# Context rows' gates of the even layer: one store of 256 reordered columns in place of three

## The chip, the cores and the metric

One core of a Trainium2 chip. The time is that of one execution of the whole program on the device, in microseconds (us); lower is better. The program is float32 throughout; matrix products are made of three float32r products of high and low parts.

## What is computed

The reference is one inference step of a two-layer backbone over 1024 latent tokens and 256 context tokens of width 1024. Cut to the even layer's gates:

```python
def even_ctx(h, w_in, w_out, gq, gk, sink):
    qa, ka, va, ga, qb, kb, vb, gb = even_projections(h, w_in, gq, gk)
    oa = dense_block_attention(qa, ka, va)
    ob = dense_block_attention(qb, kb, vb, sink)
    y = jnp.concatenate([oa * jax.nn.silu(ga), ob * jax.nn.silu(gb)], axis=-1) @ w_out
```

The same stands for the latent tokens (`even_lat`), with rotary positions, a window in mixer B and the cached context keys. The odd layer is a Fourier mixer, gated in the same way. The kernel computes all of it in one launch.

## The kernel before

The 1280 tokens are ten rows of 128: rows 0 to 7 latent, 8 and 9 context. The even layer's output projection and the odd layer work on the tokens in another order than the attention does, the *stored order*: each half of the sequence is folded so that one position stands first and the rest runs backwards. `PLACE` (L43, cut at the rows into `PIECES`, L47) says, for an attention row, which stored columns its tokens become; for row 9 it is `((1153, 0, 127), (1152, 127, 1))`, counted over all 1280 columns: 127 tokens to columns 1 to 127 of stored row 9 and the last one to column 0, read from a buffer that was written backwards.

The gates are made by `gate0(ct, gi, w)` (L869): `ct` is one of eight blocks of 128 gate channels, `gi` one of three groups of tokens (`GROUPS`, L22): rows 0 to 3, rows 4 to 7, and rows 8 and 9, which is `gi == 2`. So there are eight calls with `gi == 2`, one for each channel block. In each, TensorE (PE) makes 24 matmuls into the one bank of the tag "g" (L872, by the helper at L296), ScalarE (ACT) takes tanh of half of it into a buffer `th` of zone h (L874), VectorE (DVE) multiplies (1 + tanh) with the accumulator, by `silu` (L878), into a second buffer `gs` of zone h, and SyncE (SP) stores `gs` to the DRAM tensor `gd[row, channel, ct, token]`. For `gi == 2` the first 128 columns are written as they are and the next 128 backwards, and three transfers take them to `gd`: row 8 (L894, 64 KB), row 9's columns 1 to 127 (L895, 63.5 KB in pieces of 508 bytes) and row 9's column 0 (L896, 0.5 KB in pieces of 4 bytes). For the latent groups (L880 to L890) VectorE writes the columns in stored order at once, and one transfer takes four rows.

Zone h has nine buffers of 512 columns, taken in turn (`take`, `drop`): the one that was dropped the longest time ago is taken next, and its new user waits until the old one's readers, a store among them, have finished. The raw rows of the weights go through the same zone: `load_w` (L338, from the input projection), `out_weights` (L1170, from the output projection, whose high part ScalarE makes at L316 and whose low part VectorE or GpSimd makes at L322).

The gates are filler work. A `Filler` holds them in a queue with costs, and `attend` (L1144) pumps it while it goes through the attention units: for each unit of one 128-query row and two heads it loads queries (`load_q`, L994, from the DRAM tensor `qd`), makes scores (L989, L1061), maxima and exponentials (`soft`: L1023, L1067 on VectorE, L1030 on ScalarE), and for an earlier unit the transposes (L1108), their high and low parts (L316, L1111) and the product with the values (`weigh`, L1114, L1123, L1125). The attention output is stored at L1131, the reciprocal sums by `totals` (L1077 to L1095). Other filler is the fold of the next layer's weights (L592 to L609). The order of the gate calls:

```python
    for i, nm in enumerate(order[:-1]):
        ...
            work += [gate_work(j, c, gi) for c in range(2) for gi in range(3)]
    ...
    for gi in range(3):
        for n, (jj, c) in enumerate([(int(nm[-1]), c) for nm in order[-2:] for c in range(2)]):
            fl_.add(*gate_work(jj, c, gi))
```

So for the first four channel blocks the groups come one after the other, and for the last four the context group comes last, four calls together, with loads of `w_out` around them.

The stored gates are read once, by `proj_in` (L1273): for each stored row it loads the attention output (L1278), the gates (L1281), the reciprocal sums (L1283) and the residual (L1297), on GpSimd's queue or SyncE's, and multiplies them (L1284, L1285). The pairs of rows come in the order `PAIRS` (L68), with rows 8 and 9 last.

The program is written as a stream of operations, and the framework orders the instructions of each engine at build time, by dependencies and a simulated time line (`schedule_with_timeline_sim=True`, L2053); semaphores and waits follow from it.

Of the kernel before, what the change touches and what calls it, by code (L numbers as in the profile page):

```python
# [17 lines left out]
P = 128  # L18
# [128 lines left out]
def hybrid_step(ctx: ExitStack, tc: tile.TileContext, I, O):  # L147
    nc = tc.nc
    pe, act, dve, pool, sp = nc.tensor, nc.scalar, nc.vector, nc.gpsimd, nc.sync
# [13 lines left out]
    def take(tag, shape, dt=F32):  # L163
        tags = (tag,) if isinstance(tag, str) else tag
        z = min((t for t in tags if spare[t]), key=lambda t: spare[t][0])
        i = spare[z].popleft()[1]
        size = 2 if dt == BF16 else 4
        for s in shape[1:]:
            size *= s
        assert size <= 4 * ZONES[z][1]  # L170
        made[0] += 1
        return Buf(z, i, up.tile(list(shape), dt, tag=f"{z}{i}", name=f"{z}{made[0]}", bufs=1))

    def drop(*bufs):
        for b in bufs:
            stamp[0] += 1
            spare[b.zone].append((stamp[0], b.idx))

    def bank(tag, name, dt=F32):
        tag = ALIAS.get(tag, tag)  # L180
        return pp.tile([P, 512], dt, tag=tag, name=name, bufs=BANKS[tag])
# [6 lines left out]
    def next_bank(name):  # L188
        ring.rotate(-1)
        return bank(ring[-1], name)  # L190
# [5 lines left out]
    gd = dr.tile([NT, P, 8, P], F32, name="gd")  # L196
# [92 lines left out]
    def mm3(out, terms, lo=0, hi=None):  # L289
        n = 3 * len(terms)  # L290
        hi = n if hi is None else hi
        i = 0
        for lh, ll, rh, rl in terms:
            for a, b in ((lh, rh), (lh, rl), (ll, rh)):
                if lo <= i < hi:
                    last = pe.matmul(out, a, b, start=i == 0, stop=i == n - 1)  # L296
                i += 1
        return last
# [64 lines left out]
    def wk(w, k, c0, n):  # L363
        h, l = w[k // 4]
        return h[:, k % 4, c0 : c0 + n], l[:, k % 4, c0 : c0 + n]
# [137 lines left out]
    def hcols(gi, k, c0, n):  # L503
        kper, slots = hT[gi]
        h, l = slots[k // kper]
        return h[:, k % kper, c0 : c0 + n], l[:, k % kper, c0 : c0 + n]
# [362 lines left out]
    def gate0(ct, gi, w):  # L869
        t0, n, v = GROUPS[gi]  # L870
        acc = bank("g", f"ga{ct}{gi}")[:, 0 : n * P]
        mm3(acc, [(*wk(w, k, (ct % 2) * P, P), *hcols(gi, k, 0, n * P)) for k in range(8)])  # L872
        th = take("h", (P, n * P))
        act.activation(th.a, acc, AF.Tanh, scale=0.5)  # L874
        gs = take("h", (P, n * P))

        def silu(out, i, x):
            dve.scalar_tensor_tensor(out=out, in0=i, scalar=1.0, in1=x, op0=ALU.add, op1=ALU.mult)  # L878

        if gi < 2:  # L880
            lo = slice(0, 257) if gi == 0 else slice(256, 512)
            hi = slice(257, 512) if gi == 0 else slice(1, 256)
            if gi == 0:
                silu(gs[:, 0:257], th[:, lo], acc[:, lo])
                silu(gs[:, 257:512][:, ::-1], th[:, hi], acc[:, hi])
            else:
                silu(gs[:, 0:1], th[:, 0:1], acc[:, 0:1])
                silu(gs[:, 1:257][:, ::-1], th[:, lo], acc[:, lo])
                silu(gs[:, 257:512], th[:, hi], acc[:, hi])
            sp.dma_start(gd[t0 : t0 + 4, :, ct, :].rearrange("r p n -> p r n"), gs.a.rearrange("p (r n) -> p r n", r=4))  # L890
        else:
            silu(gs[:, 0:P], th[:, 0:P], acc[:, 0:P])
            silu(gs[:, P : 2 * P][:, ::-1], th[:, P : 2 * P], acc[:, P : 2 * P])
            sp.dma_start(gd[8, :, ct, :], gs[:, 0:128])  # L894
            sp.dma_start(gd[9, :, ct, 1:P], gs[:, 128:255])  # L895
            sp.dma_start(gd[9, :, ct, 0:1], gs[:, 255:256])  # L896
        drop(th, gs)

    HZ[0] = S1_H
# [293 lines left out]
    def gate_work(j, c, gi):  # L1193
        return (5.3 if gi < 2 else 2.7, lambda: gate0(2 * j + c, gi, ws[f"g{j}"]))
# [335 lines left out]
    for c in range(4):  # L1530
        wn = load_w(I["w_g1"][c + 1], tags=BIG) if c in (1, 2) else None
        todo = []
        for c2 in range(2):
            ct = 2 * c + c2
# [387 lines left out]
    for n, (c0, w) in enumerate(pieces):  # L1922
        sl = slice(c0, c0 + w)
        acc = next_bank(f"of7{n}")[:, 0:w]
# [136 lines left out]
```

## Time and profile before

| what | value |
|---|---|
| time, median of 3 runs (lowest to highest) | 1180.46 us (1175.72 to 1181.36) |
| time of the profiled execution | 1181.93 us |
| its span, first to last instruction | 1180.1 us |
| TensorE busy | 1151.1 us, 98% |
| VectorE busy | 829.7 us, 70% |
| ScalarE busy | 570.2 us, 48% |
| GpSimd busy | 329.8 us, 28% |
| DMA packets, of these under 512 bytes | 112592, 25946 |
| mean DMA rate | 143 GB/s |

The profile is of one execution. A row of a timeline or of the chain of waits begins with its start and its length in us; a row of a group of instructions gives the line, the engine, the operation, output and inputs, shapes and the count, then the total time in us and the mean in ns of one, then the idle time of the engine before them and what ended it. "SPq" is SyncE, which only issues transfers and waits. PEclk is the granted clock of TensorE as a share of full speed, DMA share the mean busy share of 16 DMA engines.

### The profile page before, as it was taken

The page shows a single profiled execution, that of the slowest core. Times are in us where ns is not written, and L with a number is a line of the kernel's source. Part 1 is how long each engine was busy: PE and PEld are TensorE (multiplying, and loading weights), DVE is VectorE, ACT ScalarE, POOL GpSimd, SP SyncE. Part 2 cuts the span into 40 slices and gives each one's busy share as a digit, 9 for nine tenths or more (in the row PEclk, how much of TensorE's full clock was granted, in tenths as well). Part 3 has the DMA queues.
Part 4 walks back from the last instruction along what each step waited for, and adds up shares of the span by engine and source line. Part 5 has one row for each costly group of instructions (what it writes and reads, how often), then busy time and mean ns, then how long its engine had stood idle before and what let it go on. Part 6 is the DMA issues. An engine that isn't in the chain of part 4 may idle for free.

```text
span 1180.1 us, 22034 instructions
## 1 busy us (share of the span) xinstructions
PE 1151.1 (98%) x8120; PEld 1035.5 (88%) x8120; DVE 829.7 (70%) x1996; ACT 570.2 (48%) x1149; POOL 329.8 (28%) x293
## 2 busy tenths in 40 slices
PE   9998999999999999999999989999999999999997
PEld 8797999999999998899989878887777889998886
DVE  3589787877777776678888877776765962468543
ACT  4343466565656655556666674432363234342211
POOL 2345733512222230010110035365221226200001
PEclk9999999999999999999999999999999999999999
DMA  9977412323532232344352587784214426364321
GB/s 368 371 275 256 129 62 68 97 83 101 151 90 79 77 97 85 94 127 117 78 154 78 158 227 211 232 238 162 90 46 143 151 98 181 100 213 146 125 107 54
DMA packets 112592, 168.80 MB, mean 143 GB/s; under 512 B 25946, under 2 KB 63574, under 8 KB 112484
## 3 DMA queue, kind: packets, MB, share of 16 engines
q1 hardware_dynamic: 109972, 158.74, 42.6%
q0 software_dynamic: 2368, 8.39, 2.4%
q8 instruction: 64, 1.05, 0.4%
q14 instruction: 44, 0.36, 0.1%
q10 hardware_dynamic: 144, 0.26, 0.1%
HBM read 123.19 MB, written 44.16 MB: 142 GB/s over the span
## 4 chain that ended last, share of the span: by engine, by line
PE 70%; DMA 13%; DVE 8%; issue 3%; POOL 2%; ACT 2%; SPq 1%; POOLq 0%; DVEq 0%; ACTq 0%
PE of L296 9%; PE av L1114 9%; PE pt L1108 8%; PE ga L296 8%; PE q L296 8%; PE sL L989 5%; PE u L296 5%; PE g1O L296 3%; PE kv L296 3%; PE sC L989 2%; PE g1E L296 2%; PE oz L296 2%; DMA u<-i_x 2%; DMA wd<-u 2%; PE g1c L296 1%
## 5 line engine op out<-in xcount | busy, mean ns | idle before, releaser
L1111 DVE TENSOR_TENSOR pt<-pt,pt 128x512 fp32r<-128x512 f32 (+1 forms) x264 | 170.9, 658 | 40.5 <-ACT pt L316 39.5
L316 ACT ACTIVATE pt<-pt 128x512 fp32r<-128x512 f32 (+1 forms) x265 | 147.5, 576 | 101.8 <-PE pt L1108 56.2
L1114 PE MATMUL av<-pt,u 128*128 128x256 f32 x1008 | 167.5, 290 | 1.4 <-DVE e L1125 0.8
L1108 PE MATMUL pt<-identr,p 128*128 128x128 f32 x1008 | 157.2, 273 | 1.5 <-ACT p L1030 0.8
L296 PE MATMUL q<-w,u 128*128 128x256 f32 x960 | 145.1, 287 | 0.5 <-ACT e L559 0.5
L1114 PEld LDWEIGHTS av<-pt,u 128*128 128x128 f32 x1008 | 139.1, 190 | 5.0 <-DVE e L1125 1.0
L296 PEld LDWEIGHTS q<-w,u 128*128 128x128 f32 x960 | 127.2, 189 | 5.5 <-ACT e L559 0.7
L1030 ACT ACTIVATE p<-p,nm 128x1280 f32<-128x1280 f32 (+1 forms) x80 | 95.4, 1193 | 68.2 <-DVE p L1023 68.0
L1108 PEld LDWEIGHTS pt<-identr,p 128*128 128x128 f32 x1008 | 119.7, 141 | 8.1 <-ACT p L1030 1.0
L296 PE MATMUL ga<-u,w 128*128 128x512 f32 (+1 forms) x576 | 124.4, 360 | 0.8 <-DVE byp L1085 0.5
L296 PEld LDWEIGHTS ga<-u,w 128*128 128x128 f32 x576 | 93.8, 188 | 15.4 <-ACT pt L316 1.2
L322 POOL TENSOR_TENSOR w<-h,w 128x512 fp32r<-128x512 f32 x38 | 50.0, 1331 | 134.6 <-DVE w L318 106.6
L989 PE MATMUL sL<-u,q 128*128 128x512 f32 x256 | 82.3, 409 | 0.0
L1030 ACT ACTIVATE p<-p,NM 128x640 f32<-128x640 f32 (+2 forms) x80 | 59.2, 740 | 31.5 <-DVE p L1023 31.2
L989 PE MATMUL sC<-u,q 128*128 128x256 f32 x320 | 62.1, 294 | 2.3 <-DMA q<-qd 2.0
L1023 DVE TENSOR_SCALAR_CACHE_REDUCE p<-sL 128x512 f32<-128x512 f32 x64 | 43.8, 685 | 22.3 <-PE sL L989 14.0
L1023 DVE TENSOR_SCALAR_CACHE_REDUCE p<-sL,nm 128x512 f32<-128x512 f32 x64 | 47.7, 745 | 13.9 <-PE sL L989 12.8
L296 PE MATMUL oz<-u,w 128*128 128x512 f32 x192 | 56.4, 399 | 0.4 <-DVE e L1125 0.4
L759 POOL TENSOR_TENSOR h<-h,rope 128x512 f32<-128x512 f32 (+1 forms) x18 | 21.6, 1199 | 121.4 <-ACT h L842 79.2
L989 PEld LDWEIGHTS sC<-u,q 128*128 128x128 f32 x320 | 48.8, 189 | 5.9 <-issue 2.6
L322 POOL TENSOR_TENSOR u<-h,u 128x512 fp32r<-128x512 f32 x16 | 21.0, 1323 | 109.1 <-ACT u L316 81.2
L296 PE MATMUL of<-u,u 128*128 128x512 f32 x150 | 48.2, 393 | 0.0
(735 smaller groups left out, 2590.7 us busy)
## 6 DMA issues: line engine op xcount, KB each, us to landing
q<-qd SPq DMA_DIRECT2D x80, 256.0 KB
h<-i_w_in SPq DMA_DIRECT2D x40, 256.0 KB
h<-i_w_out SPq DMA_DIRECT2D x32, 256.0 KB
p<-i_ada_s SPq DMA_DIRECT2D x11, 512.0 KB
qd<-pt SPq DMA_DIRECT2D x20, 256.0 KB
qd<-q SPq DMA_DIRECT2D x18, 256.0 KB
w<-i_wuT SPq DMA_DIRECT2D x8, 512.0 KB
u<-i_x SPq DMA_DIRECT2D x8, 512.0 KB
```

Of the source, the lines that this page charges most:

```text
L296: last = pe.matmul(out, a, b, start=i == 0, stop=i == n - 1)
L316: return act.activation(out, in_, AF.Copy)
L322: return pick("lo" + lc, lc).tensor_sub(dst_l, src, dst_h)
L759: pick("rope", XE["rope"]).tensor_mul(t1.rearrange("p t h (b c) -> p t (h b) c", b=2), y.rearrange("p t h (b c) -> p t (h b) c", b=2), cb)
L989: pe.matmul(ps, q_at(q, s, hc), keys, start=s == 0, stop=s == 1)
L1023: dve.tensor_scalar(p[i][:, end[i] : end[i] + n], ps, sign, last[i], op0=ALU.mult, op1=ALU.min, accum_out=c)
L1030: act.activation(p[i][:, 0 : end[i]], p[i][:, 0 : end[i]], AF.Exp, bias=last[i], scale=-1.0, accum_out=SU[:, t, hd + i, 0:1],)
L1108: pe.transpose(tp[:, jj * 256 + i * P : jj * 256 + i * P + P], p[i][:, off : off + P], ident)
L1111: dve.tensor_sub(pt[:, 1, 0:n], tp[:, 0:n], pt[:, 0, 0:n])
L1114: pe.matmul(acc, vv, pt[:, s, jj * 256 : jj * 256 + 256], start=c + jj + s == 0, stop=c + jj == nt - 1 and s == 1,)
```

## The change

For the context group VectorE writes the second 128 columns in stored order: column 128 of the accumulator, which belongs first, by an instruction of one column, and columns 129 to 255 backwards behind it. `gs` then holds rows 8 and 9 as `gd` does, and one transfer of 128 x 2 pieces of 512 bytes (128 KB) stores both. Nothing else is edited.

```diff
         else:
             silu(gs[:, 0:P], th[:, 0:P], acc[:, 0:P])
-            silu(gs[:, P : 2 * P][:, ::-1], th[:, P : 2 * P], acc[:, P : 2 * P])
-            sp.dma_start(gd[8, :, ct, :], gs[:, 0:128])
-            sp.dma_start(gd[9, :, ct, 1:P], gs[:, 128:255])
-            sp.dma_start(gd[9, :, ct, 0:1], gs[:, 255:256])
+            silu(gs[:, P : P + 1], th[:, P : P + 1], acc[:, P : P + 1])
+            silu(gs[:, P + 1 : 2 * P][:, ::-1], th[:, P + 1 : 2 * P], acc[:, P + 1 : 2 * P])
+            sp.dma_start(gd[8:10, :, ct, :].rearrange("r p n -> p r n"), gs[:, 0:256].rearrange("p (r n) -> p r n", r=2))
         drop(th, gs)
```

## The prediction

> **What bounds the kernel now.** I read the page's totals first, then the busy time by stretches, then the waits of TensorE, then the chain of waits where TensorE idles, and last SyncE's issues in that place.
>
> ```profile
> span 1180.1 us, 22034 instructions
> PE 1151.1 (98%) x8120; PEld 1035.5 (88%) x8120; DVE 829.7 (70%) x1996; ACT 570.2 (48%) x1149; POOL 329.8 (28%) x293
> L894 SPq DMA_DIRECT2D gd<-h x4: 326/477/592, 476.1 to 564.1; - x4
> L894 SPq DMA_DIRECT2D gd<-h x4: 319/346/403, 669.5 to 690.0; - x4
> ```
>
> TensorE (PE) is busy for 98% of the span, so a saving elsewhere is worth something only where TensorE idles. The last two rows are the store of L894, asked for in two windows: of the eight blocks that the change touches, four store between 476 and 564 us and four between 669 and 690 us. The next fence gives the busy time of each engine in the first stretch, the second, a part of the second, and the stretch behind it.
>
> ```profile
> core 0: us, PE busy (x) PEld busy (x) DVE busy (x) ACT busy (x) POOL busy (x), PEclk, DMA share, GB/s
> 440.00:660.00 220.00, 218.66 (x1422) 197.18 (x1421) 169.02 (x503) 135.89 (x291) 22.68 (x19) 1.00 0.40 107
> 660.00:710.00 50.00, 45.66 (x337) 42.36 (x336) 39.30 (x126) 34.31 (x86) 13.04 (x15) 1.00 0.71 196
> 692.00:710.00 18.00, 15.98 (x105) 14.54 (x104) 15.27 (x48) 13.96 (x35) 7.86 (x9) 1.00 0.91 244
> 710.00:760.00 50.00, 47.99 (x259) 41.38 (x258) 37.04 (x89) 23.59 (x51) 21.04 (x17) 0.97 0.72 216
> ```
>
> TensorE idles 220.00 − 218.66 = 1.34 us in the first stretch, 50.00 − 45.66 = 4.34 us in the second, and 50.00 − 47.99 = 2.01 us in the fourth. So the first four blocks stand under a full TensorE, the last four beside 4.34 us of idle time. What ends that idle time stands in TensorE's timeline, in brackets:
>
> ```profile
> 663.51 3.02 PE L296 MATMUL ga<-u,w 128*128 128x256 f32 x24 [0.31 <-DVE h L878]
> 680.55 1.64 PE L1114 MATMUL av<-pt,u 128*128 128x256 f32 x9 [0.80 <-DVE e L1125]
> 690.22 1.97 PE L609 MATMUL wa<-h,w 128*128 128x256 f32 x8 [0.39 <-ACT pt L316]
> 702.51 0.47 PE L989 MATMUL sC<-u,q 128*128 128x256 f32 x2 [1.56 <-DMA q<-qd]
> 707.00 0.71 PE L989 MATMUL sC<-u,q 128*128 128x256 f32 x4 [0.46 <-DMA q<-qd]
> ```
>
> The chain of waits shows what stands behind the last four (start, length, what):
>
> ```profile
> 670.35 3.28 DMA gd<-h
> 673.77 5.21 DMA h<-i_w_out
> 679.01 0.03 ACT u L316
> ...
> 684.04 0.47 SPq L896
> 684.56 0.02 SPq L1170
> ...
> 684.61 4.07 DMA h<-i_w_out
> 688.70 0.03 ACT u L316
> ...
> 692.25 9.60 DMA q<-qd
> ```
>
> A buffer of zone h that held gates is used again for raw rows of w_out. The load into it (L1170) waits until the store of the gates has landed, ScalarE stands in its queue at L316 for that load, and the softmax work behind it feeds TensorE late: the 0.80 and the 0.39 us. The 1.56 and 0.46 us belong to query loads (L994). SyncE's issues around it:
>
> ```profile
> 669.50 0.33 SPq L894 DMA_DIRECT2D gd<-h  x1
> 669.92 0.38 SPq L895 DMA_DIRECT2D gd<-h  x1
> 670.35 0.42 SPq L896 DMA_DIRECT2D gd<-h  x1
> ...
> 674.20 0.38 SPq L592 DMA_DIRECT2D w<-i_wuT  x1
> ...
> 680.28 0.32 SPq L896 DMA_DIRECT2D gd<-h  x1
> ...
> 689.95 0.32 SPq L894 DMA_DIRECT2D gd<-h  x1
> 690.36 0.62 SPq L895 DMA_DIRECT2D gd<-h  x1
> 691.04 0.42 SPq L896 DMA_DIRECT2D gd<-h  x1
> 691.55 0.58 SPq L1131 DMA_DIRECT2D od<-e  x1
> 692.25 1.60 SPq L994 DMA_DIRECT2D q<-qd  x2
> ```
>
> **The change part by part.** *VectorE: one instruction more in each of eight blocks.* The second product, 128 columns, becomes one of 1 and one of 127. Rows by shape of L878 between 440 and 710 us (total, mean ns), and the two products of the fifth block in VectorE's timeline:
>
> ```profile
> L878 DVE SCALAR_TENSOR_TENSOR h<-h,ga 128x128 f32<-128x128 f32 x16 | 3.7, 273 | 3.2 <-ACT h L874 3.2
> L878 DVE SCALAR_TENSOR_TENSOR h<-h,ga 128x1 f32<-128x1 f32 x8 | 1.2, 148 | 1.2 <-ACT h L874 1.2
> ...
> 669.19 0.48 DVE L878 SCALAR_TENSOR_TENSOR h<-h,ga 128x128 f32<-128x128 f32 x2
> ```
>
> The 1-column form takes 148 ns by the rows of the latent groups, and 127 columns should cost the 273 ns of 128. That is 8 x 0.148 = 1.18 us of VectorE, which is busy 169.02 of 220 us and 39.30 of 50 us there: it hides beside TensorE's own work. Its cover is gone where the next gate product waits for the single bank that the products read; that happened once, for 0.31 us (at 663.51). Bounds: nothing, and 8 x 0.148 = 1.2 us if it were so in every block. I take 4 x 0.07 = 0.3 us, half of each instruction in the second stretch, since it overlaps the neighbours in part.
>
> *SyncE: two issues fewer in each block.* They last 0.33 to 0.62 us with 0.05 us between them, about 0.43 us each: 16 x 0.43 = 6.9 us of SyncE's time, half of it in the second stretch. In the first stretch this is worth nothing, TensorE having only 1.34 us to give. In the second:
>
> Block at 669.5: the load at 673.77 waited for the third store, issued at 670.35 and 3.28 us under way. The single store can go when the third product is done; the two products end at 669.19 + 0.48 = 669.67, and a third adds about 0.1 us, so its issue falls at about 669.8. Its landing has no row. The nearest are this 0.5 KB store with 3.28 us and the 256 KB loads with 4.07 and 5.21 us. A 128 KB store stands between them in size and is nearest to the store in kind, so I take 3.28: the slot is free at 673.08 and not 673.63, 0.55 us earlier. With 4.07 it is 673.87, a loss of 0.24.
>
> [...]
>
> Block at 677.8: SyncE was held up in it twice, as its own waits between 660 and 712 us show.
>
> ```profile
> SPq L994 <- DMA q<-qd: 2.2, 1, 2.2
> SPq L1170 <- DMA gd<-h: 1.9, 1, 1.9
> SPq L896 <- DMA w<-i_wuT: 0.9, 1, 0.9
> SPq L895 <- DMA h<-i_w_out: 0.8, 1, 0.8
> ```
>
> The stores need nothing of w_uT or w_out. In the issues, the load of w_uT at 674.20 is exactly eight of SyncE's transfers before the store at 680.28: at most eight are under way, and the ninth waits for the first. So each transfer taken out frees a place as well. Nothing on TensorE hung on this block: 0, and not below.
>
> Block at 683.1: the chain goes over the third issue itself (684.04) to the load at 684.61. With one issue instead of three, and a third product ahead of it, the load goes 0.86 − 0.15 = 0.7 us earlier. ScalarE, which waited for it until 688.70, is free that much earlier, and TensorE's 0.39 us at 690.22 goes; the rest of the 0.7 meets no idle time. Gain 0.39, at least 0.
>
> Block at 690: the query loads at 692.25 stand behind three stores and one other. Two issues fewer bring them 0.43 + 0.43 + the odd 0.2 of the long one = about 0.9 us forward, less 0.15 for the product: 0.75. TensorE waited 1.56 us for them; what is late next is the transfer itself, 9.60 us long. In 692 to 710 us the DMA engines are 0.91 busy, so part of an earlier issue is spent in waiting behind GpSimd's row loads, 512 KB each and 9.4 us from issue to landing:
>
> ```profile
> w<-gd POOLq DMA_DIRECT2D x3, 512.0 KB, 9.4
> ```
>
> Bounds 0 and 1.56 + 0.46 = 2.02; I take 0.75.
>
> Sum: −0.55 (of the 0.80) −0.39 −0.75 + 0.3 = −1.39, say −1.4 us. Behind 710 us TensorE is 96% busy again, so what it gains is kept. The profiled execution took 1181.93 us, 1.83 of it outside the span of 1180.1; that gives 1180.5 for it. It lies 1.5 us above the median of the three runs, 1180.46; against the median the forecast is 1179.1.
>
> **The rivals.** *A. As above*: 0.5 to 4 us less, the end at 0.80 + 0.39 + 2.02 + a little more behind it. 1176.5 to 1180.
>
> *B. Hidden altogether.* ScalarE's wait is set by the landing of w_out (5.21 us behind 512 KB of w_uT) and TensorE's by full DMA engines. For it: the 0.91; against it: at 684 the issue itself is the chain. The extra product is left: 1180.46 + 0.3 to + 1.2 = 1180.8 to 1181.7.
>
> *C. All of the idle time comes back.* SyncE waits for the landing of gate stores in other places too, and more places under way ease every transfer in 660 to 760 us; a denser order of work falls out. Then 4.34 + 2.01 = 6.35 us go: 1174.1. Against it: the waits with the large prices (1.56, 0.80) have other transfers behind them. [...]
>
> *D. Slower, by another order of transfers.* The order on each engine is written at build time from simulated readiness, and two transfers fewer and a product more shift it from 476 us on. The price is at 692 to 710 us: the query loads share engines that move 244 GB/s with rows of 512 KB. Each row that gets ahead of them costs 524 KB / 244 GB/s = 2.15 us of TensorE waiting. Three rows ahead cost 6.4 us: 1186.9. From three on it decides; one or two end within 0.5%. For it: nine tenths busy. Against it: GpSimd issues many of these rows on a queue of its own, when buffers come free, not when SyncE does.
>
> **How the numbers follow.** Chances: A 0.55, B 0.18, C 0.15, D 0.12. One measurement of this kernel spreads from 1175.72 to 1181.36, half a per cent, 5.9 us; that is what can be told from no change. C alone reaches past it on the fast side and D alone on the slow side, so faster 0.15, same 0.73, slower 0.12. The likeliest is 1179.1. The range takes in C's 1174.1 and most of D: 1173 to 1185.5; A's own range is 1176.5 to 1180, widened by the spread of the runs.
>
> **What would show it.** L895 and L896 have gone and one store stands in their place, eight times; L878 has eight instructions more, 16 of one column in all; transfers issued by SyncE are 16 fewer. The step at 669.5 is right if the w_out load behind it is issued about 3.4 us after the store's own issue; wrong if the store takes 4 us or more. The step at 690 is right if the query load behind it follows the store at once and TensorE's wait for q falls under 1 us. TensorE's idle time in the 50 us behind the fifth block should be near 3 us. The prediction is wrong if that idle time grows, if a wait of over 2 us for q, scd or od appears on TensorE, or if time is lost where no gate is stored, which would be the order.

## The result: 0.6% slower, and the profile after

The changed kernel takes 1186.36 us, median of 12 runs (1181.34 to 1199.22), beside 1177.89 us for the kernel before in the same session (12 runs, 1175.01 to 1184.29). The ratio is 1.0064, 95% interval [1.0045, 1.0083]; ratios here are of fast runs alone, without the slow one of 1199.22 us, and the two medians as they stand would make 1.0072. Timed once more (run e18 below) the ratio is 1.0069 [1.0043, 1.0095]. The forecast was 1179.1 with a range of 1173 to 1185.5; 1186.36 lies above it, and within 0.6 us of rival D's 1186.9.

The profiled execution took 1193.25 us, 6.9 above the median. First its totals, then its stretches (columns as in the prediction), then the same two late stretches of the kernel before:

```profile
span 1191.3 us, 22014 instructions
PE 1156.4 (97%) x8120; PEld 1041.7 (87%) x8120; DVE 837.2 (70%) x2004; ACT 571.3 (48%) x1149; POOL 328.2 (28%) x293
660.00:710.00 50.00, 42.52 (x305) 39.82 (x304) 37.69 (x122) 31.86 (x77) 10.86 (x12) 0.95 0.66 190
692.00:710.00 18.00, 12.52 (x70) 11.55 (x70) 11.39 (x31) 9.22 (x21) 4.42 (x4) 0.85 0.91 257
710.00:760.00 50.00, 48.25 (x267) 41.52 (x267) 42.72 (x93) 25.79 (x57) 22.58 (x20) 0.99 0.66 195
760.00:810.00 50.00, 50.00 (x269) 42.59 (x268) 42.39 (x73) 18.38 (x48) 29.38 (x16) 1.00 0.73 229
810.00:860.00 50.00, 44.90 (x189) 35.67 (x189) 28.91 (x37) 12.94 (x20) 17.35 (x11) 0.93 0.40 136
```

```profile
760.00:810.00 50.00, 49.62 (x256) 41.37 (x255) 41.22 (x62) 16.12 (x39) 29.83 (x15) 1.00 0.69 206
810.00:860.00 50.00, 49.16 (x228) 39.50 (x226) 32.68 (x50) 18.92 (x36) 22.11 (x16) 1.00 0.39 139
```

TensorE lost time in two places: between 660 and 710 us, where the last four gate blocks lie, and between 810 and 860 us, where no gate is stored. Its waits from 660 to 1000 us, and the timeline rows of the three long ones:

```profile
PE sC L988 <- DMA q<-qd: 6.3, 2, 5.5
PE oz L296 <- DVE w L322: 3.6, 2, 2.1
PE oz L296 <- DVE h L1307: 3.0, 1, 3.0
```

```profile
705.39 0.77 PE L988 MATMUL sC<-u,q 128*128 128x256 f32 x2 [5.48 <-DMA q<-qd]
836.91 0.73 PE L296 MATMUL oz<-u,p 128*128 128x512 f32 x2 [3.01 <-DVE h L1307]
839.74 0.80 PE L296 MATMUL oz<-u,w 128*128 128x512 f32 x1 [2.10 <-DVE w L322]
```

To compare executions I use three marks on TensorE, taken from the records of the trace: the start of its 433rd product for the tile ga (635.6 us before), of its 265th for oz (798.5), and of its 49th for g1E (890.5). The **first place** is the stretch between the first two marks, the **second place** that between the last two. Before they are 162.8 and 92.1 us; in the changed kernel 164.8 and 97.5. That is 2.0 + 5.4 = 7.4 us, near the 7.5 us that 1.0064 makes of 1177.89. (So close an agreement is luck: the first place varies by several us between executions, as the table below shows.) The rest of the profile's surplus, 4.0 us, is there at the first mark already, where the two programs still run the same order: TensorE's granted clock was 0.83 of full speed from 95 to 115 us, against 1.00 (the row of this stretch, before and then after). It is not the change's; in e18, the same program, the first mark stands at 635.2 us.

```profile
95.00:115.00 20.00, 16.84 (x229) 14.78 (x228) 17.49 (x45) 4.94 (x12) 11.15 (x11) 1.00 0.73 245
95.00:115.00 20.00, 16.20 (x202) 14.07 (x202) 14.25 (x41) 5.12 (x12) 7.88 (x8) 0.83 0.62 216
```

The built programs hold the same order on every engine up to about 660 us, and from about 870 us on. Between, 22 places differ on GpSimd, 55 on SyncE, 85 on ScalarE, 161 on VectorE and 603 on TensorE.

### The profile page after: what moved, and what is told of

It is laid out like the page before. It is cut to its first block, busy times and chain, and to the rows that moved or that the text cites. A ratio compares the mean times of both kernels' runs of the same rounds, so it can differ in the third digit from the quotient of the medians.

```text
span 1191.3 us, 22014 instructions
## 1 busy us (share of the span) xinstructions
PE 1156.4 (97%) x8120; PEld 1041.7 (87%) x8120; DVE 837.2 (70%) x2004; ACT 571.3 (48%) x1149; POOL 328.2 (28%) x293
## 3 DMA queue, kind: packets, MB, share of 16 engines
q8 instruction: 64, 1.05, 0.4%
## 4 chain that ended last, share of the span: by engine, by line
PE 80%; DMA 9%; DVE 4%; issue 2%; ACT 2%; POOL 2%; SPq 1%; POOLq 0%; DVEq 0%; ACTq 0%
PE of L296 9%; PE av L1113 9%; PE q L296 9%; PE ga L296 8%; PE pt L1107 8%; PE sL L988 5%; PE oz L296 5%; PE u L296 4%; PE g1E L296 3%; PE g1O L296 3%; PE kv L296 3%; PE sC L988 3%; PE g1c L296 1%; PE sB L1060 1%; DMA q<-qd 1%
## 5 line engine op out<-in xcount | busy, mean ns | idle before, releaser
L296 PE MATMUL q<-w,u 128*128 128x256 f32 x960 | 145.1, 287 | 0.5 <-ACT e L559 0.5
L296 PEld LDWEIGHTS q<-w,u 128*128 128x128 f32 x960 | 127.2, 189 | 5.5 <-ACT e L559 0.7
L296 PE MATMUL ga<-u,w 128*128 128x512 f32 (+1 forms) x576 | 124.2, 360 | 0.3 <-DVE h L878 0.3
L296 PEld LDWEIGHTS ga<-u,w 128*128 128x128 f32 x576 | 93.7, 188 | 14.5 <-ACT pt L316 0.5
L322 POOL TENSOR_TENSOR w<-h,w 128x512 fp32r<-128x512 f32 x38 | 50.1, 1335 | 134.8 <-DVE w L318 105.1
L296 PE MATMUL oz<-u,w 128*128 128x512 f32 x192 | 57.0, 401 | 3.6 <-DVE w L322 3.6
L1022 DVE TENSOR_SCALAR_CACHE_REDUCE p<-sL 128x512 f32<-128x512 f32 x64 | 43.9, 685 | 21.1 <-PE sL L988 12.8
L322 POOL TENSOR_TENSOR u<-h,u 128x512 fp32r<-128x512 f32 x16 | 21.0, 1318 | 108.5 <-ACT u L316 104.2
L296 PE MATMUL of<-u,u 128*128 128x512 f32 x150 | 48.1, 393 | 0.0
```

Source lines behind the costliest of these rows:

```text
L322: return pick("lo" + lc, lc).tensor_sub(dst_l, src, dst_h)
L1022: dve.tensor_scalar(p[i][:, end[i] : end[i] + n], ps, sign, last[i], op0=ALU.mult, op1=ALU.min, accum_out=c)
```

## Experiments

Theory O: the loss is the other build-time order. Theory E: the edit itself costs. To part them, the order of each engine was made a part of the kernel: the instructions of each engine are chained by order-only dependencies in a stored order, that of the kernel before or that of the changed one, whole or in parts. No run times the chaining by itself; e2, chained, loses as much as the changed kernel without it, so the chaining is not what removes the loss.

```diff
+    def keep_order():                       # called at the end of the program
+        ...                                 # chain: one engine's instructions, in the stored order
+            for a, b in zip(chain, chain[1:]):
+                tc.add_manual_dep(
+                    b, a.name, mybir.DependencyInfo(mybir.DependencyClass.NoSync, mybir.DependencyReason.DATA), reason="order"
+                )
```

Line numbers in these kernels are 6 higher for the helpers (L296 is L302, L318 is L324, L322 is L328) and 25 higher in the body (the changed kernel's L1283 is L1308, L1284 is L1309, L1307 is L1332).

| run | edit | order (first part / from about 800 us) | ratio to before, 95% interval | first, second place us | longest wait for q us |
|---|---|---|---|---|---|
| e1 | yes | before / before | 0.9989 [0.9972, 1.0006] | 154.5, 90.2 | 0.4 |
| e2 | no | changed / changed | 1.0077 [1.0052, 1.0103] | 169.7, 98.2 | 6.7 |
| e3 | yes | changed / before | 1.0017 [0.9998, 1.0037] | 158.4, 90.9 | 3.1 |
| e4 | yes | before / changed | 1.0047 [1.0024, 1.0069] | 159.7, 98.1 | 2.9 |
| e5 | yes | before / SyncE changed | 1.0042 [1.0024, 1.0059] | 158.9, 95.4 | 2.5 |
| e6 | yes | before / GpSimd changed | 1.0031 [1.0010, 1.0053] | 159.4, 96.3 | 2.2 |
| e7 | yes | before / VectorE, TensorE, ScalarE changed | 0.9977 [0.9959, 0.9996] | 158.6, 90.3 | 1.9 |
| e8 | yes | SyncE, GpSimd changed / before | 1.0008 [0.9992, 1.0025] | 160.0, 90.8 | 0.5 or less |
| e9 | yes | changed / as e7 | 1.0014 [0.9992, 1.0037] | 160.9, 90.2 | 3.0 |
| e10 | no | as e7 | 0.9986 [0.9964, 1.0007] | 159.2, 89.3 | 1.6 |
| e11 | yes | as e7 | 0.9981 [0.9959, 1.0002] | 155.6, 90.9 | 1.0 |
| e12 | yes | VectorE, TensorE, ScalarE changed / the same | 1.0069 [1.0041, 1.0096] | 166.8, 90.6 | 4.5 |
| e13 | yes | e11 with one move on SyncE | 1.0046 [1.0028, 1.0064] | 157.2, 97.6 | 0.5 or less |
| e14 | yes | e11 with one move on GpSimd | 1.0045 [1.0025, 1.0064] | 162.7, 96.6 | 1.6 |
| e15 | yes | e11 with another move on GpSimd | 0.9985 [0.9968, 1.0002] | 158.1, 91.2 | 1.5 |
| e16 | yes | e9 with one move on GpSimd | 1.0005 [0.9991, 1.0018] | 161.6, 89.8 | 2.6 |
| e17 | yes | changed, but two moves | 1.0005 [0.9985, 1.0026] | 159.0, 91.7 | 3.0 |
| e18 | yes | the changed kernel again | 1.0069 [1.0043, 1.0095] | 161.5, 97.5 | 2.8 |

**The order or the edit: e1 and e2.**

> The edit (one product more, one store for three), with every engine's instructions held in the order that the kernel before has. Theory O (the loss is the other order that the build makes of the program between 660 and 870 us; the edit itself gains what the prediction's steps said): 1 to 2 us less than before, ratio 0.998 to 1.000, and TensorE's wait for the query load near 700 us at 0.5 to 1.5 us. Theory E (the added product or the larger store costs the time in any order): 7 us more than before, ratio about 1.006.

> The kernel before, unedited (two products, three stores), with every engine's instructions held in the order that the changed kernel has. Theory O: 7 to 10 us more than before, ratio 1.006 to 1.009, with a wait of about 5 us on TensorE for the query load near 700 us. Theory E: as before, ratio 0.998 to 1.002.

Medians 1177.6 and 1188.62 us. The edit in before's order loses nothing; the unedited kernel in the changed kernel's order loses all that the changed kernel lost, with its waits (8.8 us for q in all, then 3.1 and 2.1 us at oz) in the same places. Theory E has fallen.

**Which of the two places: e3 and e4.**

> The edit, in the changed kernel's order up to about 800 us and in the order of before from there. By the traces the first part lost 3.9 us in the wait for the query load and 3.4 us in a lower clock behind it, and gave some back later, the second part lost 5 us in waits of the rows 8 and 9 and 3.4 us in the clock. Theory O with the loss in the first part: ratio 1.004 to 1.007; with the loss in the second: 0.998 to 1.001. Theory E: 1.006.

> The edit, in the order of before up to about 800 us and in the changed kernel's order from there. Theory O with the loss in the first part: ratio 0.998 to 1.001; with the loss in the second: 1.004 to 1.007. Theory E: 1.006.

Both count. Against e1, the new order costs 0.28% in the first part alone, little more than the noise of two such timings, and 0.58% in the second alone. The second place is read without doubt, as its stretch scatters little: 98.1 us with the new order there, 90.9 without.

**Which engine in the second place: e5, e6, e7.**

> The edit with the order of before on every engine, except that behind about 800 us SyncE alone issues in the changed kernel's order: there the store of x1d stands ahead of the load of od for row 9. The whole second part in the new order cost 0.58% (1184.1 against 1177.6). Theory S (SyncE's queue makes the loss at 833 us: the load waits in the queue behind a store whose data come late, so row 9's rows land some 6 us later, and everything that uses them follows): 1183 to 1185, ratio to before about 1.0045, and waits of TensorE at oz for VectorE of 3 to 7 us near 833. Theory H (the loss is made where GpSimd, VectorE and TensorE stand in line behind an operation that is not ready): 1177 to 1179, ratio 0.998 to 1.001, no wait of over 1.5 us at oz.

> The edit with the order of before, except that behind about 800 us GpSimd alone works in the changed kernel's order: row 8's product ahead of row 9's, and the small product for the root of rows 4 and 5's squares ahead of the cast that makes row 9's high part. Theory S (SyncE's queue): nothing, 1177 to 1179. Theory H: GpSimd holds row 9's high part back until the small product is ready, VectorE's low part and TensorE's oz for row 9 wait for it: 1180 to 1184, with a wait of 2 to 6 us on TensorE at oz near 833. If only VectorE's and TensorE's order matter, 1177 to 1179 here and the loss in the next run.

> The edit with the order of before, except that behind about 800 us VectorE, TensorE and ScalarE work in the changed kernel's order: VectorE makes row 9's low part (L322) only behind the odd-and-even sums of the pair before and row 8's low part, and TensorE takes the whole product of row 8 ahead of row 9. SyncE and GpSimd as before. Theory S: nothing, 1177 to 1179. Theory H: row 9 was ready first and now waits in VectorE's line for operations that are not ready; TensorE waits at oz for 3 to 8 us near 833: 1181 to 1185.

Against e1's 90.2 us, SyncE's new order alone costs 5.2 us of the stretch, GpSimd's alone 6.1, the three computing engines' nothing. (The stored orders differ there in seven places on SyncE and nine on GpSimd.) Theory S was near for e5, but TensorE's wait was 2.45 us, below its 3 to 7, and the load that it named, row 9's od, is not the one that e13 moves. Theory H was right for GpSimd (e6), but wrong where I held VectorE's order for the cause: e7 in that order is the fastest kernel of all.

**The single moves: e13, e14, e15.** In `proj_in` a row's gates are multiplied with the scaling (scd, the reciprocal sums) and then with the attention output (od); gtd holds the gate rows of the layer's output, x1d the layer's result, and r12y is a reciprocal root made of the squares of an earlier pair of rows. Names with a number are single buffers. On SyncE, the second half of a scaling load (u<-scd, row 9) goes behind three others; on GpSimd, row 8's product goes ahead of row 9's (e14), or the small product r12y ahead of row 9's cast (e15).

```diff
 SyncE (e13)
-u<-scd, second half, row 9
 w<-gtd
 w<-od, row 9
 x1d<-pt
+u<-scd, second half, row 9
```

```diff
 GpSimd (e14)
+w1089: row 8's product
 w1098, p1101, u1116: row 9's product and cast, a low part of w_g
-w1089: row 8's product
 r12y, p1092: the small product, row 8's cast
```

```diff
 GpSimd (e15)
 w1098: row 9's product
+r12y
 p1101, u1116, w1089
-r12y
 p1092
```

> The kernel of e11 with one move on SyncE: the second half of row 9's scaling load (u<-scd) is issued behind the gate-row load, row 9's od load and an x1d store, which stood behind it. In e5 the load went at 803.75 instead of 799.11, and GpSimd's product for row 9 began at 811.86 instead of 803.86. If this move is what e5 showed: TensorE's stretch from oz 265 to g1E 49 is 94 to 96 us (90.3 and 90.9 without it) and the ratio to before about 1.002. If it takes the other moves of e5's order: 90 to 91 us and 0.998.

> The kernel of e11 with one move on GpSimd: row 8's product with od (w1089) stands ahead of row 9's product, cast and the next low part. Row 8's od lands later than row 9's: in e6 GpSimd stood 5.85 us for it. If that is what e6 showed: the stretch from oz 265 to g1E 49 is 93 to 97 us, TensorE waits for row 9's low part or for VectorE at oz for 2 us or more, ratio about 1.002. If the small product for the root (next run) is the cause: 90 to 91 us and 0.998.

> The kernel of e11 with one other move on GpSimd: the small product for the root of a pair's squares (r12y, 0.69 us) stands ahead of the cast that makes row 9's high part. It waits for a sum that follows TensorE's oz of the pair before (r12x, at about 814 us), while row 9 is ready at 810.5. If this is what e6 showed: GpSimd waits 3 to 5 us at r12y, the stretch is 93 to 96 us and the ratio about 1.001. If the swap of the products is the cause: 90 to 91.5 us and 0.998.

One move on SyncE alone costs 97.6 − 90.9 = 6.7 us, one on GpSimd alone 5.7 us; moving r12y costs nothing. The rows show how. GpSimd's timeline in the kernel before (product of row 9 with the scaling, with od, cast), then in the changed kernel:

```profile
810.48 2.41 POOL L1284 TENSOR_TENSOR q<-q,u 128x1024 f32<-128x1024 f32 x1 [7.57 <-DMA u<-scd]
814.54 2.62 POOL L1285 TENSOR_TENSOR w<-w,q 128x1024 f32<-128x1024 f32 x1 [1.65 <-DMA w<-od]
817.22 1.04 POOL L318 CAST p<-w 128x1024 fp32r<-128x1024 f32 x1
```

```profile
823.24 2.39 POOL L1283 TENSOR_TENSOR q<-q,u 128x1024 f32<-128x1024 f32 x1 [13.82 <-DMA u<-scd]
825.59 2.40 POOL L1284 TENSOR_TENSOR w<-w,u 128x1024 f32<-128x1024 f32 x1
827.94 2.40 POOL L1284 TENSOR_TENSOR w<-w,q 128x1024 f32<-128x1024 f32 x1
830.30 0.69 POOL L275 TENSOR_TENSOR r12y<-r12x,mhalf 128x2 f32<-128x2 f32 x1
830.94 2.04 POOL L318 CAST p<-w 128x1024 fp32r<-128x1024 f32 x2
```

And SyncE's issues there, before and then changed:

```profile
802.06 0.49 SPq L1283 DMA_DIRECT2D u<-scd  x1
806.24 1.15 SPq L1283 DMA_DIRECT2D u<-scd  x1
807.49 0.53 SPq L1383 DMA_DIRECT2D w<-gtd  x1
```

```profile
808.03 0.49 SPq L1282 DMA_DIRECT2D u<-scd  x1
812.18 1.21 SPq L1382 DMA_DIRECT2D w<-gtd  x1
813.48 0.38 SPq L1409 DMA_DIRECT2D x1d<-pt  x1
814.22 0.32 SPq L1277 DMA_DIRECT2D w<-od  x1
814.59 0.94 SPq L1282 DMA_DIRECT2D u<-scd  x1
```

The second half goes out 6.6 us behind the first instead of 4.2, and with row 9's od load ahead of it, it is also longer under way: row 9's first product starts 8.65 us after that issue instead of 4.24. So it starts 823.24 − 810.48 = 12.8 us later, 6.8 when the 6.0 us by which everything stood later at the second mark are taken off. In e13 the same move shows alone (issue, then the product that waits for it, 8.45 us later):

```profile
802.19 0.49 SPq L1307 DMA_DIRECT2D u<-scd  x1
810.64 2.40 POOL L1308 TENSOR_TENSOR q<-q,u 128x1024 f32<-128x1024 f32 x1 [14.65 <-DMA u<-scd]
```

Then row 8's product (w<-w,u) stands ahead of row 9's (w<-w,q). Before, row 9's cast ended 817.22 + 1.04 − 810.48 = 7.8 us after the scaling product began; now it is the second of the two casts in the last row and ends 830.94 + 2.04 − 823.24 = 9.7 us after it. That cast is not what TensorE waits for in the end, though. The changed kernel's chain of waits goes from the late products over r12y, which stands behind them on GpSimd:

```profile
830.34 0.66 POOL r12y L275
831.03 1.16 ACT w L1422
832.21 1.85 DVE u L1423
836.17 1.28 DVE h L1307 x2
837.45 2.25 DVE w L322
```

VectorE is idle for 12.28 us before L1423, which needs r12y by way of ScalarE. Behind it in VectorE's order stand L1307, which reads TensorE's accumulator (TensorE's wait of 3.0 us), and row 9's low part, L322 (its wait of 2.1 us), although the cast for that was done at 832.98. The chains of e13 and e14 run the same way. So r12y is a link of the path, and late because of the products ahead of it; e15 says only that its place before the cast does not matter. In e14, where row 9's data are early, GpSimd stands still for row 8's:

```profile
820.18 2.38 POOL L1309 TENSOR_TENSOR w<-w,u 128x1024 f32<-128x1024 f32 x1 [5.61 <-DMA w<-od]
833.44 1.22 PE L302 MATMUL oz<-u,p 128*128 128x512 f32 x2 [3.58 <-DVE h L1332]
```

**The two moves undone in the changed kernel: e9, e17, e18.**

> The changed kernel with its own order on every engine, but for the second part (from about 800 us) on SyncE and GpSimd, where 10 and 8 places are put back as they stood before. Theory Q (the loss at 833 us is made by these two engines alone): TensorE's stretch from oz 265 to g1E 49, 97.5 us in the changed kernel, is 90 to 91 us here, and the time comes back to before's or nearly: ratio 0.998 to 1.002. The rival of it, that the loss needs VectorE's order too, would leave 93 us or more and 1.003 to 1.006. What is left over the repeat of e7 in this call is the price of the first part: 0 if that was chance, 0.2 to 0.3% (2 to 3.5 us) by the runs so far.

> The changed kernel in its own order on every engine, with two moves: on SyncE the second half of row 9's scaling load goes back ahead of the gate-row load, the x1d store and row 9's od load, and on GpSimd row 9's product and cast go back ahead of row 8's product. If these two are the loss near 833 us: TensorE's stretch from oz 265 to g1E 49 is 90 to 91 us instead of 97.5, and the ratio to before 1.000 to 1.002, as e9 had with 18 places put back. If other moves carry a part: 92 us or more, and 1.003 to 1.005.

```diff
 SyncE (e17)
+u<-scd, second half, row 9
 w<-gtd
 x1d<-pt
 w<-od, row 9
-u<-scd, second half, row 9
```

```diff
 GpSimd (e17)
+w1098, p1101: row 9's product and cast
 w1089: row 8's product
-w1098: row 9's product
 r12y, p1092
-p1101: row 9's cast
```

> The changed kernel as it is, once more. By its first timing 1.0045 to 1.0083. Near 700 us, if the new order itself brings TensorE's wait for the query load: 3 to 7 us again; if the 5.5 us were chance: 0.4 to 3 us as in the kernels with before's order there. Near 833 us the stretch from oz 265 to g1E 49 is 97 to 98 us again.

In e9, with both engines' whole second part put back, the second place is 90.2 us and the ratio 1.0014. With these two moves alone put back, the changed kernel's ratio falls from 1.0069 to 1.0005 in the same session (1185.44 to 1178.66 us) and the second place from 97.5 to 91.7 us. TensorE's waits from 810 to 860 us in e18, then in e17:

```profile
PE oz L296 <- DVE h L1307: 3.1, 1, 3.1
PE oz L296 <- DVE w L322: 1.7, 1, 1.7
```

```profile
PE oz L302 <- DVE w L328: 1.0, 1, 1.0
PE oz L302 <- DVE h L1332: 0.7, 1, 0.7
```

**The first place: e8, e12, e16.** In e16 the load of gd for row 1 stands behind row 0's products:

```diff
 GpSimd (e16)
-w961<-gd, row 1
 u929<-gd, row 0
 u929, w962<-scd, u928: row 0's products and half a load
+w961<-gd, row 1
```

The q wait in the changed kernel was 5.48 us the first time and 2.79 in e18, the same program both times, so 2.7 us of it were chance. What remains is small: the six profiles with the edit and the whole new order there (after, e3, e9, e16, e17, e18) average 161.0 us, the nine with the edit and before's order (e1, e4, e5, e6, e7, e11, e13, e14, e15) 158.3. The timings say the same: e3 against e1 0.28%, e9 against e11 0.33%.

> The edit with the order of before, except that between about 660 and 800 us the two engines that issue transfers, SyncE and GpSimd, work in the changed kernel's order; VectorE, TensorE and ScalarE keep that of before. With all engines in the new order in this part, 1179.5, and a wait of 3.1 us (5.5 in the changed kernel, 6.7 in the unedited kernel with that order) on TensorE for the query load. Theory G (the row loads of GpSimd, issued in one bunch ahead of the query load, take the DMA engines from it): the wait for q is over 3 us here too, 1179 to 1182. Theory K (the query load is late because the work that frees its buffer is late in the other engines' order): the wait for q stays under 1 us, 1177 to 1179.

> The edit with VectorE, TensorE and ScalarE in the changed kernel's order throughout, and SyncE and GpSimd in before's order throughout. Theory K (in the first part the loss comes from the order of the computing engines, by freeing the query's buffer late or holding TensorE behind VectorE): 0.2 to 0.3% slower than e11. Theory G (it comes from the issue order, GpSimd's row loads ahead of the query load): as e11, ratio 0.997 to 0.9995, and TensorE's wait for q under 2.5 us.

> The kernel of e9 (the changed kernel's order in the first part) with one move on GpSimd: the load of gd for row 1 (w961, 512 KB) is issued behind row 0's two products instead of ahead of them, so it no longer shares the DMA engines with the query loads that are issued in the same us. Theory G (the rows ahead of the query load make TensorE's wait, 2.15 us a row): the wait for q falls from 3.0 to 0.5 to 1.5 us and the query load lands 1.5 to 2.5 us sooner after its issue; the time falls by 1 to 2 us at most, 1.0 to 1.001, if row 1 isn't late instead. Rival (the queues of the two engines are served apart, or the transfers of SyncE itself are the ones ahead): the wait stays at 2.5 to 3.5 us.

e8 has the changed kernel's bunch of row loads, and its query loads went out between them, without a wait for q over 0.5 us: theory G, that the issue order alone makes the wait, is not borne out by this run. e12 has the computing engines' new order with the old issue orders, and is worse than e8 and than e9, which has the whole new order in this part (its waits for q are 4.5 and 2.3 us). Both signs of theory K came, e8 without a wait and e12 slower than e11; but e12 lost 0.9% where K said 0.2 to 0.3, so most of e12's loss is that the computing engines' order and the issue orders don't fit each other. e16 bounds the price of a row: with one 512 KB row moved behind, the wait falls from 2.98 (e9) to 2.58 us and the time from the second query load's issue to its use from 11.30 to 10.57 us. Theory G's 2.15 us a row is not there, and the wait stays where the rival put it; the other runs with the whole new order have 10.8 to 11.3 us (14.1 in the changed kernel's first profile), so that even the 0.7 us are at the edge of what single profiles tell.

```profile
696.77 0.47 PE L1013 MATMUL sC<-u,q 128*128 128x256 f32 x2 [2.98 <-DMA q<-qd]
698.35 0.48 PE L1013 MATMUL sC<-u,q 128*128 128x256 f32 x2 [2.58 <-DMA q<-qd]
```

What the 2.7 us of the first place consist of, the same fifteen traces tell: TensorE's waits for q come to 3.7 us on average with the new order and 1.6 with before's, and half of its busy time at half the granted clock to 1.1 and 0.6 us. That is 2.1 + 0.5 = 2.6 us. Why the queries come late in the new order stays open: e8 shows that the issue orders alone don't make these waits, and e12's waits are longer than those of the whole new order.

**The edit alone, and the fastest order: e10, e11.**

> The unedited kernel (three stores, two products) with the order of e7: before's, but VectorE, TensorE and ScalarE in the changed kernel's order from about 800 us on. Against the repeat of e7 in this call it has the edit alone undone. Theory V (the edit saves 1.4 us as the prediction summed it, up to 2): 0.1 to 0.2% slower than e7, ratio to before 0.998 to 1.001. Theory N (the edit is worth nothing, and what e7 gained came from VectorE's order): as e7 within 0.05%. Theory C (all idle time of the part comes back): 0.4% or more slower than e7.

> e7 again, beside the runs that it is compared with: the edit with before's order, but VectorE, TensorE and ScalarE in the changed kernel's order from about 800 us on. If e7's gain is real: ratio 0.996 to 0.9995, 1173 to 1177. If it was chance: 0.999 to 1.001.

In one and the same order the edited kernel takes 1176.52 us and the unedited 1176.87: 0.03%, which these intervals cannot tell from nothing. The edit with e7's order is the fastest version seen, 0.9977 and 0.9981 in two timings of 12 runs, some 0.2% under before; the second interval takes in 1.

## Why the prediction was wrong, step by step

**The step that failed** is the ground of case A: that the work stays in the order of before, so that the sum can be made wait by wait. The prediction named the rival, that two transfers fewer and a product more shift the build-time order, and gave it 0.12. e1 and e2 show that this rival is the whole result. That its total was near (1186.9 against 1186.36) is luck. It put everything at 692 to 710 us, three rows at 2.15 us each; and it added 6.4 us to the median of three runs, 1180.46, where twelve runs give 1177.89 and the medians differ by 8.5 us. Near 700 us the order cost about 3 us, and a row moved away gave 0.7 us in e16 (0.4 of the wait). The larger part, over 5 us, lies 130 us later. "Time lost where no gate is stored, which would be the order" was named as the sign, and it came; its place and mechanism were not foreseen.

**The terms of the sum** were about right where they can be seen. The changed kernel's chain of waits, for the fifth block's store and the w_out load behind it, and for the query load of the block at 690:

```profile
673.68 3.15 DMA gd<-h
676.85 3.85 DMA h<-i_w_out
690.60 0.69 SPq L993
691.34 13.92 DMA q<-qd
```

- Block at 669.5: the single 128 KB store takes 3.15 us, the 0.5 KB one took 3.28, where 3.28 was assumed; the load goes out 3.17 us after the store's issue (about 3.4 was named). What short pieces cost, the two stores don't tell, as one is 256 times the other in size.
- VectorE's extra instruction: 8 more one-column forms at 147 ns, and 278 ns for 127 columns (148 and 273 assumed). TensorE's wait for L878 is the same 0.3 us.

```profile
L878 DVE SCALAR_TENSOR_TENSOR h<-h,ga 128x1 f32<-128x1 f32 x16 | 2.4, 147 | 1.2 <-ACT h L874 1.2
L878 DVE SCALAR_TENSOR_TENSOR h<-h,ga 128x127 f32<-128x127 f32 x8 | 2.2, 278 | 0.0
```

- Blocks at 669.5 and 683: the traces show the gain. The changed kernel stood 4.1 us behind at TensorE's 481st ga product (663.5 us before) and 2.2 us behind at its 105th wa product (694.8): 1.9 us gained, where −0.55 and −0.39 were forecast for these blocks. It is the edit's own: the stretch between these two products takes 31.3, 31.2 and 30.4 us in the three profiles without the edit (before, e2, e10) and 29.3 us on average, 28.4 to 30.8, in the seventeen with it, whatever the order.
- Block at 690: the query load did come earlier, at 690.60 against 692.25, though TensorE stood more than 2 us behind. But that is the new order's doing and not that of two issues fewer: the load now stands ahead of this block's store, which goes out at 693.00. And what "is late next" came true at once: the second query load took 13.92 us instead of 9.60 (10.8 to its use in e18), and TensorE waited longer. 0.75 of gain became a loss. TensorE's idle time from 660 to 710 us, forecast near 3 us for the 50 us behind the fifth block, was 50.00 − 42.52 = 7.5 us.

**The rivals.** B (at most 1181.7) and C (1174.1) fall with A. That the edit by itself is worth 1.4 us of the whole time is neither shown nor refuted: its stretch is 1.6 us shorter, but e10 and e11 give 0.4 us for the whole, with intervals of about 2.5 us each way.

## What to carry to other kernels

Where the order on each engine is made at build time, an edit's price is the sum of its parts only if the order holds; compare the built orders first, and price the places that differ, however far from the edit. Pinning the old order under the new code, and the new order under the old code, takes two runs and parts the edit from the order. Look then for queues in which something ready stands behind something that is not: here one load, and one row's product and cast, out of place made nearly all of the loss, among some 900 places that differed.

## What the runs showed of the hardware

In e18 a pause of TensorE cost more than its own length. The wait of 3.06 us ends at 829.35 us; 6.8 us at a granted clock of 0.50 follow, and the wait of 1.70 us lies within them:

```profile
829.50:836.30 6.80, 5.10 (x12) 3.51 (x13) 6.31 (x8) 1.76 (x4) 1.56 (x2) 0.50 0.55 193
836.50:846.00 9.50, 9.50 (x43) 7.71 (x42) 6.85 (x10) 2.02 (x3) 1.90 (x2) 1.00 0.15 57
```

By estimate half of the 5.10 us busy there is lost, 2.6 us; with the waits of 3.1 + 1.7, less the 1.0 + 0.7 that e17 has, this gives 5.7 us, and the stretches differ by 97.5 − 91.7 = 5.8. A stretch at a lower clock is in each of the profiles with a long second place. From 810 to 860 us the granted clock is 0.93 in after, e6 and e18 and 0.97 in e5. TensorE's longest wait at oz there was 2.45 us in e5 and 2.32 us in e6. In e2, e4, e13 and e14 pairs of oz products of 1.05 to 1.06 us stand in the ten us behind the longest wait, and pairs of 0.62 to 0.63 us after them. Of the profiles with a short second place, before, e1, e7, e8, e9, e11 and e17 have a clock of 1.00 from 810 to 860 us.

The length of the pause does not decide it alone. In e3 and e17 TensorE waited 3.1 and 3.0 us for q, and the eight av products behind it took 1.20 us; in e18 it waited 2.8 us, and they took 1.89 us. In e7 it waited 1.9 us, and four av products soon after took 1.20 us, where the next four took 0.72; the clock from 660 to 710 us was 0.97 in e7 and e18. What decides it, these runs do not show.
